# One hybrid decoder layer on one core: reciprocals of the softmax sums taken before they are turned, one weight load traced ahead of the copies, casts behind exponentials, two halves in one step

## The chip, the core and the metric

The kernel runs on one core of a Trainium2 chip. The metric is the device time of one execution in microseconds (us); the time of a kernel is the median of its runs. A core has a matrix engine (PE, with its weight loads shown as PEld), a vector engine (DVE), a scalar engine (ACT), a general engine (POOL) and SyncE (SP), which here mostly issues DMA transfers. Every engine takes its own instructions strictly in the order in which they stand, and waits on semaphores for what the others make.

## The reference

One decoder layer over 1024 positions of width 1024, all float32. Both attention groups read one normalised input; group A has 8 query heads over 2 key heads in a window of 128 with a sink logit, group B has 8 heads with a learned decay.

```python
xn = rmsnorm(x, attn_norm_g)
proj = jnp.einsum('bsd,de->bse', xn, w_in)
qa, ka, va, qb, kb, vb, f_logit = jnp.split(proj, IN_SPLITS, axis=-1)
# q and k of both groups are RMS-normalised per head of 64
out_a = swa_sinks_attention(qa, ka, va, sink_logits)   # exp(s-m) / (sum + exp(sink-m)) @ v
out_b = forgetting_attention(qb, kb, vb, log_f)        # softmax(s + c[t] - c[s]) @ v
x = x + jnp.einsum('bse,ed->bsd', concatenate([out_a, out_b]), w_out)
hn = rmsnorm(x, mlp_norm_g)
hid = jnp.square(jax.nn.relu(jnp.einsum('bsd,df->bsf', hn, w_up)))
return x + jnp.einsum('bsf,fd->bsd', hid, w_down)
```

## The kernel before, in words

Every large product is made of three: an operand is **split** into a rounded high part (a cast, by ACT or DVE) and a low remainder (a subtraction, by DVE or POOL), and high*high, high*low and low*high are added in PSUM. `split` (L75) does it for weights.

The program has these stages.

1. **First projection** (L177 to L227): 8 row tiles (`qps0` to `qps7`, all 8 PSUM banks) of the first 384 columns of the input projection. The results are copied to `q0`, even tiles by DVE and odd ones by ACT (L225 to L227).
2. **Second projection** (`wa1_tile`, L455): 392 more columns, 8 tiles of 24 products each, with weights that `load_w` (L237) brings: for each of 8 slices a DMA into `wr`, a cast `w` by ACT, a low part `w` by POOL. Results go to two PSUM buffers (`ps`, pool `pd`), from which ACT copies them to `q3` and `z`. Meanwhile `qknorm` (L266) squares `q0` and `q3` on POOL (`sq`), sums on DVE (`ss`) and scales on POOL, and the q and k parts are turned by PE (`ptq`, `ptk`, L331) and split (`q1a`, `k1a`, `k2z`).
3. **Attention of group A** (`scores_a`, `mix_a`; 16 units), then **group B** in four pairs of heads p = 0 to 3 (`scores_b`, `mix_b`; 8 units each). A unit makes scores `sp`/`spb` on PE, adds a bias with a running minimum on DVE (`sa`, `sb`, `nm`), an exponential with its sum on ACT, and two units later turns the probabilities on PE (`tpa`, `tpb`, L565 and L740), evicts them split (`pth` by ACT, `ptl` by DVE, L402 and L403), multiplies by v (`pv`, `pvb`) and sends the result (`mta`, `mtb`, two buffers of the tag "mt") to DRAM (`mix_d`). The turned tiles of all these steps, and that of the sums, share **three PSUM buffers of the tag "tr"**. Between them PE works on fillers: the 8 tiles of the next pair's projection (`project_b`, `ps`) and, during p = 3, the first half of the output projection (`out_first`, `po`).
4. **Sums.** For group A and for p = 0 to 2 the probabilities are not divided at once: the sums lie in `dn_a` or `dn_b`, one column for each head and tile of 128 queries. `inverse_to` (L583) turns them on PE (`ptn`), takes reciprocals on DVE (`rd`, tag "mt") and stores them to `rd_d`. `split_mix(e)` (L602) later loads a row block of `mix_d` (`mixr`) and the broadcast reciprocals (`mixn`), and in two steps, one for each half of 512, multiplies them on DVE (L624), splits the product (ACT and POOL, `mixs`) and stores it to `mixs_d`, from where `load_mix` brings it as an operand of the output projection. Pair p = 3 is divided in place (L711 to L718).
5. **Output projection and both MLP products** (from L957): the MLP in a seven-product scheme of 512-column blocks, bound to PE from end to end.

The order on each engine is not written out. The code is traced with priorities (`high_priority`, by which a block is taken earlier), and a scheduler places each instruction when its model of the engines finds it ready. `issue_after(i)` puts the block's instructions that run on i's engine behind i in that engine's order and adds no wait. `PACE` says at which unit a filler is let in, and `SPLITS` after which unit each `split_mix` starts: its load at once, its steps one by one after the next units.

Of the kernel before, what the change touches and what calls it, by code (L numbers as in the profile page):

```python
# [8 lines left out]
F32 = mybir.dt.float32  # L9
# [3 lines left out]
ALU = mybir.AluOpType  # L13
AX = mybir.AxisListType
PSUM = bass.MemoryType.PSUM

P = 128
D = 1024
S = 1024
KT = D // P  # L20
NT = S // P
HD = 64
NH = 8
# [15 lines left out]
LAST = (6, 7, 0, 1, 2, 3, 4, 5)  # L39
# [16 lines left out]
def hybrid_layer(  # L56
# [13 lines left out]
    nc = tc.nc  # L70

    def mm(out, lhsT, rhs, start, stop):
        return nc.tensor.matmul(out, lhsT, rhs, start=start, stop=stop)  # L73

    def split(hi, lo, src, hi_eng, lo_eng):  # L75
        if hi_eng is nc.scalar:
            hi_eng.copy(hi, src)  # L77
        else:
            hi_eng.tensor_copy(hi, src)
        return lo_eng.tensor_tensor(out=lo, in0=src, in1=hi.bitcast(F32), op=ALU.subtract)  # L80

    def rsqrt(pool, out, t, shape, tag):
# [11 lines left out]
    cp = ctx.enter_context(tc.tile_pool(name="cp", bufs=1))  # L94
# [3 lines left out]
        out=ident, in_=ident, pattern=[[-1, P]], compare_op=ALU.not_equal,  # L98
# [4 lines left out]

    vt = cp.tile([P, 68], F32, name="vt")
    gm, vec, bfb, snk = (
        vt[:, a:b] for a, b in ((0, 8), (8, 12), (12, 20), (20, 28))
    )
# [53 lines left out]
    ap2 = at.enter_context(tc.tile_pool(name="ap2", bufs=1, side="right"))  # L163

    ap3 = at.enter_context(tc.tile_pool(name="ap3", bufs=1, side="right"))
    qk_t = lambda name: ap1.tile([P, NT, 384], F32, tag="qk", name=name, bufs=2)
# [10 lines left out]
    st0 = ExitStack()  # L177
    ps0 = st0.enter_context(tc.tile_pool(name="ps0", bufs=1, space=PSUM))
    qps = [ps0.tile([P, 512], F32, name=f"qps{t}") for t in range(NT)]
# [5 lines left out]
    for k in range(KT):  # L185
        xr = ap2.tile([P, S], F32, tag="s", name="xr", bufs=NS)

        wr, wh, wl = w_tiles(384)
# [15 lines left out]
        for cs in pieces:  # L204
# [3 lines left out]
                out=lo, in0=xr[:, cs], scalar=ga,  # L208
# [9 lines left out]
        for t, j in order:  # L218
# [2 lines left out]
                qps[t][:, :384], x_part(part_, k, slice(t * P, (t + 1) * P)), w_,  # L221
                k == 0 and j == 0, k == KT - 1 and j == 2,
            )
    q0 = qk_t("q0")
    for t in LAST:  # L225
        eng = (nc.vector.tensor_copy, nc.scalar.copy)[t % 2]
        eng(q0[:, t, :], qps[t][:, :384])  # L227
    st0.close()

    psa = ExitStack()  # L230
    pa = psa.enter_context(tc.tile_pool(name="pa", bufs=1, space=PSUM, reuse_waits="tile"))
    psd = ExitStack()
    pd = psd.enter_context(tc.tile_pool(name="pd", bufs=2, space=PSUM, reuse_waits="tile"))

    copied, squared = [], []

    def load_w(src, n):  # L237
        his, los = [], []
        for k in range(KT):
            wr, wh, wl = w_tiles(n)  # L240
            nc.sync.dma_start(wr[:, :n], src[:, k, :])
            with ExitStack() as behind:
                for ins in (copied[-1], squared[-1]) if copied and k > 2 else ():
                    behind.enter_context(tc.issue_after(ins))
                behind.enter_context(tc.high_priority(offset=HPO))
                split(wh, wl, wr[:, :n], nc.scalar, nc.gpsimd)
            his.append(wh)
            los.append(wl)
        return his, los

    middle = []

# [13 lines left out]
    def qknorm(x, nh, tlo, thi, r=None):  # L266


        n = thi - tlo
        w = nh * HD  # L270
        ss, r0, u = (
            ap3.tile([P, 16], F32, tag=tag, name=tag, bufs=2)[:, : n * nh]
            for tag in ("ss", "sr0", "su")
        )
        m = n // 2
        for i in range(2):
            sq = ap2.tile([P, 512], F32, tag="sq", name="sq", bufs=1)[:, : m * w]
            xv = x[:, tlo + i * m : tlo + (i + 1) * m, :w]
            square = nc.gpsimd.tensor_tensor(
                out=sq.rearrange("p (t c) -> p t c", t=m), in0=xv, in1=xv, op=ALU.mult  # L280
            )
            if i == 0:
                squared.append(square.ins)
            nc.vector.tensor_reduce(
                out=ss[:, i * m * nh : (i + 1) * m * nh],
                in_=sq.rearrange("p (g d) -> p g d", d=HD), axis=AX.X, op=ALU.add,
            )
        th = lambda a: a.rearrange("p (t h) -> p t h", h=nh)
        nc.vector.scalar_tensor_tensor(
            out=th(ss), in0=th(ss), scalar=1.0 / HD,  # L290
            in1=ep2[:, tlo:thi].unsqueeze(2).to_broadcast([P, n, nh]),
            op0=ALU.mult, op1=ALU.add,
        )
        nc.scalar.activation(r0, ss, AF.Ln)
        nc.scalar.activation(r0, r0, AF.Exp, scale=-0.5)
        nc.vector.tensor_tensor(out=u, in0=r0, in1=r0, op=ALU.mult)
        nc.vector.tensor_tensor(out=u, in0=u, in1=ss, op=ALU.mult)
        na = nh + (2 if r is not None else 0)
        if r is None:
            rv = ap3.tile([P, 16], F32, tag="r", name="r", bufs=2)[:, : n * nh]  # L300
            rv = th(rv)
        else:
            rv = r[:, tlo:thi, :]
        nc.vector.scalar_tensor_tensor(
            out=rv[:, :, :nh], in0=th(u), scalar=3.0, in1=th(r0),
            op0=ALU.subtract, op1=ALU.mult,
        )
        for t in range(n):
            xt = x[:, tlo + t, : na * HD].rearrange("p (h d) -> p h d", d=HD)
            nc.gpsimd.tensor_tensor(  # L310
                out=xt, in0=xt, in1=rv[:, t].unsqueeze(2).to_broadcast([P, na, HD]), op=ALU.mult
            )
# [93 lines left out]
        return hi, lo  # L406


    wa1 = load_w(w_a1, 392)
    rt = cp.tile([P, NT], F32, name="rt")  # L410
    for t in range(NT):
        xq = ap2.tile([P, S], F32, tag="s", name="xq", bufs=NS)
# [114 lines left out]
    def scores_a(g, i):  # L527
        lo = 0 if i else P
        kr = slice(max(i - 1, 0) * P, max(i - 1, 0) * P + 256)
        pts = [  # L530
            ap2.tile([P, 2, 256], F32, tag=("u", "s")[j], name=f"sa{j}", bufs=(NU, NS)[j])
            for j in range(2)
        ]
        nm, dn = (a[:, 4 * g : 4 * g + 4, i] for a in (nm_a, dn_a))
        for h in range(2):
            sp = pa.tile([P, 2, 256], F32, tag="sc", name="sp", bufs=2)
            for j in range(2):
                qs = qa[g, j, i // 4][:, h, (i % 4) * P : (i % 4 + 1) * P]
                mm(sp[:, j, :], qs, k1a[g][:, kr], True, False)
                pe = mm(sp[:, j, :], qs, k2_of[g][:, kr], False, True)  # L540
            for j in range(2):
                hh = 2 * j + h
                n = 256 - lo
                nc.vector.tensor_tensor_reduce(
                    out=pts[j][:, h, lo:], in0=sp[:, j, :n], in1=ab[g][:, hh, lo:],
                    scale=1.0, scalar=nsnk[:, 4 * g + hh : 4 * g + hh + 1],
                    op0=ALU.add, op1=ALU.min, accum_out=nm[:, hh : hh + 1],
                )
        for hh in range(4):
            pr = pts[hh // 2][:, hh % 2, lo:]  # L550
            nc.scalar.activation(
                pr, pr, AF.Exp, scale=-1.0, bias=nm[:, hh : hh + 1],
                accum_out=dn[:, hh : hh + 1],
            )
        marks.append(pe.ins)
        return pts

# [24 lines left out]

    def inverse_to(first, dn, n):  # L583

        pt = pa.tile([P, 512], F32, tag="tr", name="ptn", bufs=3)
        nc.tensor.transpose(pt[: n * NT, :P], dn.rearrange("p h t -> p (h t)"), ident)
        rd = ap2.tile([P, 256], F32, tag="mt", name="rd", bufs=2)[: NH * NT, :P]
        nc.vector.reciprocal(rd[: n * NT], pt[: n * NT, :P])
        nc.sync.dma_start(
            rd_d[first : first + n].rearrange("h (t q) -> (h t) q", q=P), rd[: n * NT]  # L590
        )
# [10 lines left out]
    def split_mix(e):  # L602


        got = {}

        def load():
            for c in range(2):
                cs = slice(c * 512, (c + 1) * 512)
                m, q = got[c] = [  # L610
                    ap2.tile([P, 512], dt, tag=n, name=n, bufs=2)
                    for n, dt in (("mixr", F32), ("mixn", F32R))
                ]
                nc.sync.dma_start(m, mix_d[e][:, cs])
                for h in range(2):
                    nc.sync.dma_start(
                        q[rows_of[h], :].bitcast(F32), rd_d[2 * e + h, cs].partition_broadcast(HD)
                    )

        def make(c):  # L620
            m, q = got[c]
            lo = ap2.tile([P, 512], F32R, tag="mixs", name="mixs", bufs=1)
            with tc.issue_after(mixed[-1]):
                nc.vector.tensor_tensor(out=m, in0=m, in1=q.bitcast(F32), op=ALU.mult)  # L624
            split(q, lo, m, nc.scalar, nc.gpsimd)
            for part_, t in enumerate((q, lo)):
                nc.sync.dma_start(
                    mixs_d[e][part_][:, c * 512 : (c + 1) * 512], t.bitcast(F32)
                )

        return [load, lambda: make(0), lambda: make(1)]


# [784 lines left out]
```

## Time and profile before

| what | value |
|---|---|
| runs | 1082.19, 1083.85, 1083.93 us; median 1083.85 us |
| profiled execution | 1082.51 us, its span 1080.8 us (1.7 us lie around the span) |
| granted PE clock | 0.999 of full speed |
| busy in the span | PEld 930.5, DVE 780.2, ACT 573.4, POOL 383.2 us |
| instructions | PE 5492, DVE 1319, ACT 1022, POOL 350 |
| stages by time in the span | first projection to about 38 us, second to 77, group A to about 200, group B to 427, then output projection to 465, MLP up to 772, MLP down to 1078 |

A timeline row gives the start, the duration from the first start to the last end of a merged group, engine, source line, operation, output tile and inputs, shapes and the count; in brackets stands the idle time ahead of it and what ended it. PE's records overlap: a product's record is longer than the distance to the next product's start, so that PE can count as busy while it loses time. What a stall costs is read from the distance of two starts against the usual one for that shape.

### The profile page before, as it was taken

Reading aid. Unit: us, or ns where it says so; the run is one execution under the profiler, and the core shown is the slowest. Engines: PE = TensorE matmul, PEld = TensorE weight load, DVE = VectorE, ACT = ScalarE, POOL = GpSimd, SP = SyncE. Lnnn points to the kernel's source line nnn. Section 1 sums busy time; section 2 is a strip of 40 time slices with the busy share of each in tenths; the row PEclk is TensorE's granted clock in tenths of the full one; section 3 lists DMA queues with packets and bytes.
Section 4 is the critical chain, followed back from the end, with each engine's and each line's share of the span. In section 5 each row is a group of like instructions: output and inputs, shape, how many; then the busy total and the mean of one; then the engine's idle time right before and its main releaser. Section 6 shows DMA issues by size and latency. Waiting matters only on the chain.

```text
span 1080.8 us, 15581 instructions
## 1 busy us (share of the span) xinstructions
PE 1070.7 (99%) x5492; PEld 930.5 (86%) x5492; DVE 780.2 (72%) x1319; ACT 573.4 (53%) x1022; POOL 383.2 (35%) x350
## 2 busy tenths in 40 slices
PE   9999999999999999999999999999999999999998
PEld 8999999999998887888888888888888888888886
DVE  7377787877875787997777869674776876764495
ACT  5558587776767765655445453534533433333331
POOL 4572433546555663323233332322212313131100
PEclk9999999999999999999999999999999999999999
DMA  8401212324747656544454543443998885665423
GB/s 290 163 20 56 62 43 66 117 89 139 235 169 250 228 193 241 196 156 175 166 202 168 182 169 146 153 162 116 369 391 311 307 296 200 236 232 186 174 81 116
DMA packets 96366, 195.93 MB, mean 181 GB/s; under 512 B 7408, under 2 KB 19872, under 8 KB 96288
## 3 DMA queue, kind: packets, MB, share of 16 engines
q1 hardware_dynamic: 96000, 194.80, 51.2%
q8 instruction: 43, 0.70, 0.3%
q14 instruction: 35, 0.29, 0.1%
q10 hardware_dynamic: 288, 0.15, 0.0%
HBM read 141.87 MB, written 53.04 MB: 180 GB/s over the span
## 4 chain that ended last, share of the span: by engine, by line
PE 72%; DVE 2%; issue 1%; DMA 0%; ACT 0%; DVEq 0%; ACTq 0%
PE pu L73 28%; PE pd L73 28%; PE po L73 8%; PE pvb L73 2%; PE ps L73 2%; PE tpb L740 2%; PE spb L73 2%; DVE ptl L403 0%; DVE sb L699 0%; DMA mix_d<-mtb 0%; PE ptk L331 0%; DVE m L1040 0%; DVE pd L1333 0%; PE ptq L331 0%; PE pms L73 0%
## 5 line engine op out<-in xcount | busy, mean ns | idle before, releaser
L73 PE MATMUL pd<-hx,wx 128*128 128x512 f32 (+1 forms) x1350 | 304.9, 388 | 0.0
L73 PEld LDWEIGHTS pd<-hx,wx 128*128 128x128 f32 x1350 | 252.8, 188 | 52.1
L73 PE MATMUL pu<-bh,wu 128*128 128x512 f32 x896 | 276.6, 390 | 0.0
L73 PEld LDWEIGHTS pu<-bh,wu 128*128 128x128 f32 x896 | 168.2, 188 | 35.2 <-issue 0.2
L73 PE MATMUL ps<-w,x 128*128 128x384 f32 (+1 forms) x960 | 196.5, 342 | 0.6 <-ACT z L460 0.3
L73 PE MATMUL pu<-bl,wu 128*128 128x512 f32 x448 | 174.5, 389 | 0.0
L73 PEld LDWEIGHTS ps<-w,x 128*128 128x128 f32 x960 | 165.2, 188 | 4.8 <-POOL w L80 1.0
L77 ACT CAST hx<-hr 128x1024 fp32r<-128x1024 f32 x56 | 59.1, 1055 | 175.2 <-PE pd L73 171.0
L80 POOL TENSOR_TENSOR wx<-wda,wx 128x1024 fp32r<-128x1024 f32 x24 | 65.3, 2720 | 195.6 <-ACT wx L77 177.3
L80 DVE TENSOR_TENSOR hx<-hr,hx 128x1024 fp32r<-128x1024 f32 x56 | 72.3, 1299 | 71.0 <-ACT hx L77 71.0
L73 PEld LDWEIGHTS pu<-bl,wu 128*128 128x128 f32 x448 | 84.1, 188 | 18.0 <-DVE bl L978 0.3
L73 PE MATMUL po<-mix,wos 128*128 128x512 f32 x384 | 93.6, 393 | 0.0
L80 POOL TENSOR_TENSOR wu<-wus,wu 128x512 fp32r<-128x512 f32 x32 | 46.9, 1468 | 127.5 <-ACT wu L77 127.5
L73 PEld LDWEIGHTS po<-mix,wos 128*128 128x128 f32 x384 | 70.7, 188 | 13.8
L80 POOL TENSOR_TENSOR wu<-wur,wu 128x512 fp32r<-128x512 f32 x31 | 41.8, 1350 | 85.6 <-ACT wu L77 85.6
L77 ACT CAST wu<-wus 128x512 fp32r<-128x512 f32 x64 | 38.0, 618 | 58.9 <-PE pu L73 52.8
L1037 DVE TENSOR_TENSOR ht<-hb 128x512 f32<-128x512 f32 x32 | 22.9, 756 | 63.2 <-ACT hb L1145 63.2
L704 ACT ACTIVATE sb<-sb,nmb 128x128 f32<-128x128 f32 (+3 forms) x64 | 49.9, 779 | 26.3 <-DVE nmb L699 25.7
L403 DVE TENSOR_TENSOR ptl<-tpb,pth 128x512 fp32r<-128x512 f32 (+1 forms) x80 | 49.9, 630 | 17.5 <-ACT pth L402 16.6
L77 ACT CAST wx<-wda 128x1024 fp32r<-128x1024 f32 x56 | 58.5, 1049 | 7.6 <-DMA wda<-in_w_d_dram 7.6
L80 POOL TENSOR_TENSOR w<-wr,w 128x384 fp32r<-128x384 f32 (+1 forms) x47 | 49.9, 1070 | 28.6 <-ACT w L77 17.3
L694 POOL TENSOR_SCALAR_AFFINE_SELECT cm<-cb 128x128 f32<-128x128 f32 (+1 forms) x64 | 30.7, 479 | 57.5 <-DVE nmb L699 56.8
(207 smaller groups left out, 1837.7 us busy)
## 6 DMA issues: line engine op xcount, KB each, us to landing
wda<-in_w_d_dram SPq DMA_DIRECT2D x34, 1024.0 KB, 9.1
hr<-hid_d SPq DMA_DIRECT2D x56, 512.0 KB, 6.3
wur<-in_w_u_dram SPq DMA_DIRECT2D x32, 512.0 KB, 4.4
hid_d<-ht SPq DMA_DIRECT2D x16, 1024.0 KB, 4.3
hid_d<-hb SPq DMA_DIRECT2D x16, 768.0 KB, 3.6
mix<-mixs_d SPq DMA_DIRECT2D x7, 1024.0 KB, 5.8
wr<-in_w_b_dram SPq DMA_DIRECT2D x32, 192.0 KB, 2.4
xq<-in_x_dram SPq DMA_DIRECT2D x8, 512.0 KB, 5.7
```

The source lines that it names most:

```text
L73: return nc.tensor.matmul(out, lhsT, rhs, start=start, stop=stop)
L77: hi_eng.copy(hi, src)
L80: return lo_eng.tensor_tensor(out=lo, in0=src, in1=hi.bitcast(F32), op=ALU.subtract)
L403: nc.vector.tensor_tensor(out=lo[:, cols], in0=pt[:, cols], in1=hi[:, cols].bitcast(F32), op=ALU.subtract)
L694: nc.gpsimd.affine_select(out=cm, in_=bias, pattern=[[-1, n]], compare_op=ALU.is_ge, fill=BIG, base=n - P, channel_multiplier=1,)
L704: nc.scalar.activation(pr[:, :nk], pr[:, :nk], AF.Exp, scale=-1.0, bias=nm[:, c : c + 1], accum_out=dn_b[p % 2][:, h, i : i + 1] if p < 3 ...
L740: nc.tensor.transpose(tp[:, c0 : c0 + P], probs[qi][:, kb * P : (kb + 1) * P], ident)
L1037: eng.tensor_tensor(out=out, in0=a, in1=b, op=ALU.subtract)
```

## The change

Six edits:

- `load_w(w_a1)` is traced ahead of the copies of `q0`, not after them; the copies of tiles 1, 3 and 5 (on ACT) stand behind the last cast of that load, and the first square of `qknorm` (on POOL) behind its last low part.
- In the loads of the pairs' weights, the casts of slices 3 to 7 stand, besides what they stood behind, behind the last exponential of the first unit of group A (`exps[0]`) when it has been traced.
- `inverse_to` takes the reciprocals on DVE on the sums themselves, in place, before they are turned: 128 x 64 for group A and 128 x 16 for a pair, where it was 64 x 128 and 16 x 128 out of PSUM.
- The turned reciprocals are copied out of PSUM by ACT.
- They go to a tile of the tag "zes" (one buffer) and no longer to "mt" (two buffers, shared with `mta` and `mtb`).
- `split_mix(6)` makes both halves in one step. Besides, a constant tile `vt` is 28 and not 68 columns wide, of which 28 were used.

```diff
+    split_casts = []
     def split(hi, lo, src, hi_eng, lo_eng):
-        if hi_eng is nc.scalar:
-            hi_eng.copy(hi, src)
-        else:
-            hi_eng.tensor_copy(hi, src)
+        cast = (hi_eng.copy if hi_eng is nc.scalar else hi_eng.tensor_copy)(hi, src)
+        split_casts[:] = [cast.ins]
...
-                for ins in (copied[-1], squared[-1]) if copied and k > 2 else ():
+                for ins in (copied[-1], squared[-1], *exps[:1]) if copied and k > 2 else ():
...
+    wa1 = load_w(w_a1, 392)
+    last_a1 = list(split_of)
+
+    q0 = qk_t("q0")
+    for t in LAST:
+        eng = (nc.vector.tensor_copy, nc.scalar.copy)[t % 2]
+        with tc.issue_after(last_a1[0]) if t in (1, 3, 5) else nullcontext():
+            eng(q0[:, t, :], qps[t][:, :384])
...
+            with tc.issue_after(last_a1[1]) if not squared else nullcontext():
+                square = nc.gpsimd.tensor_tensor(
...
-    wa1 = load_w(w_a1, 392)
...
+        exps.append(exp.ins)
...
     def inverse_to(first, dn, n):
 
+        nc.vector.reciprocal(dn, dn)
         pt = pa.tile([P, 512], F32, tag="tr", name="ptn", bufs=3)
         nc.tensor.transpose(pt[: n * NT, :P], dn.rearrange("p h t -> p (h t)"), ident)
-        rd = ap2.tile([P, 256], F32, tag="mt", name="rd", bufs=2)[: NH * NT, :P]
-        nc.vector.reciprocal(rd[: n * NT], pt[: n * NT, :P])
+        rd = ap2.tile([P, P], F32, tag="zes", name="rd", bufs=1)
+        nc.scalar.copy(rd[: n * NT], pt[: n * NT, :P])
...
+        if e == KT - 2:
+            return [load, lambda: (make(0), make(1))]
         return [load, lambda: make(0), lambda: make(1)]
```

Three places show how the order moves. The first is POOL at the end of the first projection: `w` of 392 columns are the low parts of the second projection's weights, `sq` the squares of `q0`. Before:

```order
L80 TENSOR_TENSOR w<-wr,w 128x384 x6
L80 TENSOR_TENSOR w<-wr,w 128x392 x7
L279 TENSOR_TENSOR sq<-q_424 128x512
L80 TENSOR_TENSOR w<-wr,w 128x392
L279 TENSOR_TENSOR sq<-q_424 128x512 x2
L310 TENSOR_TENSOR q_424<-q_424,rqk 128x384 x4
```

With the change:

```order
L80 TENSOR_TENSOR w<-wr,w 128x384 x6
L80 TENSOR_TENSOR w<-wr,w 128x392 x8
L285 TENSOR_TENSOR sq<-q_464 128x512 x4
L316 TENSOR_TENSOR q_464<-q_464,rqk 128x384 x4
L285 TENSOR_TENSOR sq<-q_518 128x384
```

The eighth low part no longer stands behind a square, and all four squares of `q0` now stand ahead of its first scaling.

The second place is DVE during the pair p = 2, where the sums of p = 1 are inverted. Before, the reciprocal reads the turned tile `ptn`:

```order
L403 TENSOR_TENSOR ptl<-tpb,pth 128x512
L699 ISA sb,nmb<-spb,cm 128x128
L699 ISA nmb 128x1
L588 RECIPROCAL rd<-ptn 16x128
L403 TENSOR_TENSOR ptl<-tpb,pth 128x384
```

With the change it reads the sums, stands some 45 rows earlier on DVE, and the release of `ptn` is a copy on ACT; the first fence is DVE, the second ACT, whose casts `pth` release the other tiles of the tag:

```order
L409 TENSOR_TENSOR ptl<-tpb,pth 128x512
L591 RECIPROCAL dn_b_83<-dn_b_83 128x16
L409 TENSOR_TENSOR ptl<-tpb,pth 128x384
L764 TENSOR_TENSOR mtb<-pvb,mtb 64x256
L631 TENSOR_TENSOR mixr<-mixr,mixn 128x512
```

```order
L408 CAST pth<-tpb 128x384 x2
L713 ACTIVATE sb,dn_b_82<-sb,nmb 128x512
L595 COPY rd<-ptn 16x128
L656 COPY qkb_3501<-ps 128x384
L408 CAST pth<-tpb 128x512
```

So PE's turning of the sums now waits for DVE, and its tile is given back by ACT.

The third place is DVE near the end of group B, with the second product `mixr` of `split_mix(6)` before:

```order
L713 TENSOR_SCALAR sb<-sb,dnb 128x640
L755 TENSOR_TENSOR mtb<-pvb,mtb 64x256
L624 TENSOR_TENSOR mixr<-mixr,mixn 128x512
L403 TENSOR_TENSOR ptl<-tpb,pth 128x512
L711 RECIPROCAL dnb<-dnb 128x1
```

With the change the second product stands some 19 rows earlier, beside the first (first fence), and around the eviction `ptl` in question (second fence) none is left:

```order
L764 TENSOR_TENSOR mtb<-pvb,mtb 64x256
L631 TENSOR_TENSOR mixr<-mixr,mixn 128x512 x2
L720 RECIPROCAL dnb<-dnb 128x1
L708 ISA sb,nmb<-spb,cb_5147 128x512
L708 ISA nmb 128x1
```

```order
L409 TENSOR_TENSOR ptl<-tpb,pth 128x384
L708 ISA sb,nmb<-spb,cm 128x256
L708 ISA nmb 128x1
L720 RECIPROCAL dnb<-dnb 128x1
L722 TENSOR_SCALAR sb<-sb,dnb 128x768
L409 TENSOR_TENSOR ptl<-tpb,pth 128x512
```

On PE the fillers move with it: before, 12 products `po` stand in two groups of six on either side of eight turnings, now all 12 stand ahead of them:

```order
L73 MATMUL spb<-k2z_441,q1b_4557 128x256
L73 MATMUL po_5721<-mix_4738,wos 128x512 x3
L73 MATMUL po_5721<-mix_5146,wos 128x512 x3
L740 MATMUL tpb<-ident,sb 128x128 x8
L73 MATMUL po_5722<-mix_4738,wos 128x512 x3
L73 MATMUL po_5722<-mix_5146,wos 128x512 x3
```

With the change eleven turnings follow one another:

```order
L73 MATMUL po_5726<-mix_5149,wos 128x512
L73 MATMUL pvb<-pth,vb_4821 128x256
L749 MATMUL tpb<-ident,sb 128x128 x3
L73 MATMUL pvb<-ptl,vb_4821 128x256
L749 MATMUL tpb<-ident,sb 128x128
L73 MATMUL pvb<-pth,vb_4821 128x128
L73 MATMUL pvb<-ptl,vb_4821 128x128
L749 MATMUL tpb<-ident,sb 128x128 x11
```

In the second projection PE's first scores `sp` stand, counted over the rows, behind 99 products `ps` before and behind 115 now. The rest of the order shifts by a few rows throughout group A and group B; behind L957 hardly anything moves.

More of the change, by code (lines that the diff above doesn't have):

```diff
@@ L102, in hybrid_layer @@
     nc.vector.memset(ones1, 1.0)
-    vt = cp.tile([P, 68], F32, name="vt")
+    vt = cp.tile([P, 28], F32, name="vt")
     gm, vec, bfb, snk = (
@@ L223, in hybrid_layer @@
             )
[L224 to L235, printed above, removed]
+    copied, squared, split_of, exps = [], [], [], []
     def load_w(src, n):
@@ L242, in load_w @@
             with ExitStack() as behind:
-                for ins in (copied[-1], squared[-1]) if copied and k > 2 else ():
+                for ins in (copied[-1], squared[-1], *exps[:1]) if copied and k > 2 else ():
                     behind.enter_context(tc.issue_after(ins))
                 behind.enter_context(tc.high_priority(offset=HPO))
-                split(wh, wl, wr[:, :n], nc.scalar, nc.gpsimd)
+                low = split(wh, wl, wr[:, :n], nc.scalar, nc.gpsimd)
+            split_of[:] = [split_casts[0], low.ins]
             his.append(wh)
@@ L249, in load_w @@
         return his, los
+    wa1 = load_w(w_a1, 392)
[5 more added lines that the diff above has]
+            eng(q0[:, t, :], qps[t][:, :384])
+    st0.close()
+    psa = ExitStack()
+    pa = psa.enter_context(tc.tile_pool(name="pa", bufs=1, space=PSUM, reuse_waits="tile"))
+    psd = ExitStack()
+    pd = psd.enter_context(tc.tile_pool(name="pd", bufs=2, space=PSUM, reuse_waits="tile"))
     middle = []
@@ L278, in qknorm @@
             xv = x[:, tlo + i * m : tlo + (i + 1) * m, :w]
-            square = nc.gpsimd.tensor_tensor(
-                out=sq.rearrange("p (t c) -> p t c", t=m), in0=xv, in1=xv, op=ALU.mult
-            )
+            with tc.issue_after(last_a1[1]) if not squared else nullcontext():
+                square = nc.gpsimd.tensor_tensor(
+                    out=sq.rearrange("p (t c) -> p t c", t=m), in0=xv, in1=xv, op=ALU.mult
+                )
             if i == 0:
@@ L550, in scores_a @@
             pr = pts[hh // 2][:, hh % 2, lo:]
-            nc.scalar.activation(
+            exp = nc.scalar.activation(
                 pr, pr, AF.Exp, scale=-1.0, bias=nm[:, hh : hh + 1],
```

## Prediction

> **What bounds the kernel now.** I read first the page's busy times, then the chain that ended last, then the list of PE's waits.
>
> ```profile
> PE 1070.7 (99%) x5492; PEld 930.5 (86%) x5492; DVE 780.2 (72%) x1319; ACT 573.4 (53%) x1022; POOL 383.2 (35%) x350
> ```
>
> PE has 10.1 us of the span in which no record runs. The chain shows where it can't be moved at all:
>
> ```profile
> 426.78 38.16 PE po L73 x168
> ...
> 771.60 300.57 PE pd L73 x1326
> ```
>
> Shown are the first and the last of the four long stretches from 426.8 us on, in which products follow one another with next to nothing between them; 38.16 / 168 is 0.227 us for a product of 512 columns, which is also 300.57 / 1326. Nothing in the change touches these, so the kernel's end lies a fixed distance behind the last product of group B, and the change is worth what it takes from PE's stalls before 427 us, no more. The waits of PE:
>
> ```profile
> PE tpb L740 <- DVE ptl L403: 1.0, 1, 1.0
> PE tpb L740 <- DVE dnb L711: 0.6, 1, 0.6
> PE tpb L740 <- DVE rd L588: 0.6, 1, 0.6
> ...
> PE ps L73 <- ACT z L460: 0.3, 1, 0.3
> PE ps L73 <- POOL w L80: 0.3, 1, 0.3
> PE sp L73 <- DVE q1a L324: 0.3, 1, 0.3
> ```
>
> These are few and short, and three of these six name what the change touches. Their true size is larger, since the records overlap; I take it from the starts. The ceiling of the whole change is thus some 7 us, 0.7% of the time.
>
> **Part 1: the load ahead of the copies.**
>
> ```profile
> L73 PE MATMUL ps<-w,x 128*128 128x392 f32 x192 | 36.6, 346 | 0.6 <-ACT z L460 0.3 <-POOL w L80 0.3
> ...
> 38.36 4.07 PE L73 MATMUL ps<-w,x 128*128 128x392 f32 x22
> 42.70 0.45 PE L73 MATMUL ps<-w,x 128*128 128x392 f32 x1 [0.27 <-POOL w L80]
> ...
> 40.60 1.06 POOL L279 TENSOR_TENSOR sq<-q 128x512 f32<-128x512 f32 x1
> ...
> 41.63 1.01 POOL L80 TENSOR_TENSOR w<-wr,w 128x392 fp32r<-128x392 f32 x1
> ...
> 57.62 0.27 PE L331 MATMUL ptk<-ident,q 128*128 128x128 f32 x1
> 58.15 0.39 PE L73 MATMUL sp<-k1a,q1a 128*128 128x256 f32 x1 [0.26 <-DVE q1a L324]
> ```
>
> The first row is a group (busy us, mean ns of one record): less the 0.35 us of the last record, 22 products follow at (4.07 - 0.35) / 21 = 0.177 us, so the 23rd was due at 42.26 and came at 42.70: **0.4 us** lost, because the eighth low part stood behind a square of 1.06 us on POOL. In the new order it stands ahead of that square, and its cast ahead of two copies on ACT; POOL is free at 40.6, so it is ready near 41.6. I take the 0.4 us as gone. What is late next is the square, by some 1.1 us, and with it the scaling and turning of `q0`. The first scores `sp` came 0.53 us behind the start of a turning, which takes 0.1 at most (eight in 1.03 us, below). In the new order 115 products of the second projection stand ahead of them, where it was 99: 16 x 0.177 = 2.8 us more time for a chain that is 1.1 us later, so I count **0.5 us** as gone too. Bounds: 0 (both come back at the next buffer, as `z` L460 does above) to -0.9.
>
> **Part 2: casts behind exponentials.**
>
> ```profile
> 79.86 0.52 ACT L77 CAST w<-wr 128x384 fp32r<-128x384 f32 x1 [1.55 <-DMA wr<-in_w_b_dram]
> 80.28 0.40 ACT L551 ACTIVATE sa<-sa,nm_a 128x128 f32<-128x128 f32 x1
> ```
>
> ACT stood 1.55 us behind a weight slice that had not landed, with exponentials queued behind it. In the new order the four of the first unit stand ahead of it: 4 x 0.4 = 1.6 us, just the time that ACT stood, so the cast is hardly later than its DMA lets it be. PE's list names a low part `w` once only, that of part 1, and no exponential; I count **nothing**. The cover is PE's fillers; without them 1.6 us would be to gain, or as much to lose if the weights came late.
>
> **Part 3: the reciprocals and their tile.** `ptn` takes one of the three "tr" buffers until the reciprocal has read it.
>
> ```profile
> L588 DVE RECIPROCAL rd<-ptn x4: 935/937/946, 204.9 to 388.0; 16x128 f32<-16x128 f32 x3, 64x128 f32<-64x128 f32 x1
> ...
>   DMA mix_d<-mtb: 0.9, 1
> ...
> 201.76 0.49 PE L740 MATMUL tpb<-ident,sb 128*128 128x128 f32 x3
> 202.43 0.36 PE L73 MATMUL pvb<-pth,vb 128*128 128x256 f32 x1 [0.18 <-DVE mta L576]
> ...
> 255.19 0.27 PE L586 MATMUL ptn<-ident,dn_b 128*16 128x128 f32 x1
> ...
> 269.01 0.94 DVE L588 RECIPROCAL rd<-ptn 16x128 f32<-16x128 f32 x1
> ...
> 269.17 0.70 PE L73 MATMUL ps<-w,x 128*128 128x384 f32 x3
> 270.00 0.55 PE L740 MATMUL tpb<-ident,sb 128*128 128x128 f32 x3
> 270.61 0.38 PE L73 MATMUL pvb<-pth,vb 128*128 128x256 f32 x1
> ...
> 314.36 0.27 PE L586 MATMUL ptn<-ident,dn_b 128*16 128x128 f32 x1
> ...
> 325.97 0.40 PE L73 MATMUL spb<-k2z,q1b 128*128 128x512 f32 x1
> 326.96 0.55 PE L740 MATMUL tpb<-ident,sb 128*128 128x128 f32 x3 [0.60 <-DVE rd L588]
> ```
>
> It is held from 255.19 to 269.95, and from 314.36 to 326.9: 12 to 15 us, because `rd` waits for a buffer of "mt", and so for a store of `mtb`. PE then turns with two buffers. At 326.96 the turning was due 0.23 us after 325.97: 0.77 us lost. At 270.00 three products of 0.174 from 269.17 end at 269.69: 0.3 lost, and 0.3 more ahead of 270.61. Sum **1.4 us**. With the change `rd` has its own buffer, free since the store of a pair before, and ACT's copy stands among the `pth` casts.
>
> ```profile
> L711 DVE RECIPROCAL dnb<-dnb x16: 143/164/165, 357.4 to 415.9; 128x1 f32<-128x1 f32 x16
> ...
> L477 DVE RECIPROCAL zt<-zt x1: 553/553/553, 112.1 to 112.1; 128x64 f32<-128x64 f32 x1
> ...
> L754 ACT COPY mtb<-pvb x32: 369/370/373, 203.5 to 426.9; 64x256 f32<-64x256 f32 x32
> ```
>
> The reciprocals cost 0.55 us for 128 x 64 and, between 0.16 and 0.55, about 0.25 for 128 x 16: 1.3 us in place of 3.75 on DVE. The copies cost at most 0.37 us each, 4 x 0.37 = 1.5 us on ACT, off the path as long as ACT idles. Bounds for the part: 0 (the next buffer is as late) to -1.8, if the gap ahead of 202.43 (0.67 from the turnings' start, where three take 0.25) goes as well, where group A's `ptn` was held too but another release is named. I take -1.4, since a reader of `ptn` is named at the longest gap and ends 0.05 us ahead of the other.
>
> One rule speaks against this part: the Trainium skill, "Perfetto Trace Analysis", section "Optimizing Scalar/DVE Operations", sees offloading from VectorE to ScalarE as sensible when VectorE is saturated, and VectorE is busy 72% here. By it the copy would gain nothing, and the sum would lose its 1.4; the row of `rd` says that the buffer was held by a wait and not by load.
>
> **Part 4: both halves in one step.**
>
> ```profile
> 410.79 1.54 PE L73 MATMUL po<-mix,wos 128*128 128x512 f32 x6
> ...
> 413.92 1.44 DVE L624 TENSOR_TENSOR mixr<-mixr,mixn 128x512 f32<-128x512 f32 x1
> 415.28 0.68 DVE L403 TENSOR_TENSOR ptl<-tpb,pth 128x512 fp32r<-128x512 f32 x1
> ...
> 412.17 1.03 PE L740 MATMUL tpb<-ident,sb 128*128 128x128 f32 x8
> ...
> 416.11 0.52 PE L740 MATMUL tpb<-ident,sb 128*128 128x128 f32 x3 [0.64 <-DVE dnb L711]
> 417.63 1.16 PE L740 MATMUL tpb<-ident,sb 128*128 128x128 f32 x7 [1.00 <-DVE ptl L403]
> ```
>
> PE's two longest waits, by starts 0.86 and 1.17 us, follow from `ptl` at 415.28, which stood behind `mixr`. Without that row it starts near 413.9. But the order of the rest changes with it. Now the pair's last scores are done at 410.8, where the fillers start, and the turning that waits last starts at 417.63, 6.8 us later; without `mixr` 5.4, and with one eviction more in that time, as the new order has it, 6.1. PE then has between the two 12 x 0.227 for the fillers, which now come first, 15 turnings at 0.11 and 12 pv products of half the columns, 0.12 each: 5.8 us. That leaves a wait of 0.3; but the first three of those turnings after eight already need an eviction, and the low part of the result now follows its sum on DVE at once and must stand for ACT's cast, up to 1 us at each place. So the 2.0 us become 0.3 to 2.3. I take 1.5, nearer to the upper end, because both waits ended on DVE: **-0.5**, with bounds +0.3 and -1.7.
>
> **The sum.** -0.4 - 0.5 - 1.4 - 0.5 = -2.8. The order moves by some rows everywhere, and a handful of short waits comes and goes with it; I allow +0.3. That is -2.5 us: 1082.5 - 2.5 = 1080.0 for an execution like the profiled one. The median of the runs stands 1.3 us above that execution, so the median with the change is 1083.85 - 2.5 = **1081.3 us**, 0.23% less.
>
> **Rivals.** (a) *The waits come back at the next buffer*: a `tr` buffer is freed earlier, but the next turning then waits for `ptl` or `mtb`, as the list shows at other places; only part 1's first gap and the 0.77 stay gone, 1.2 us, less 0.3: about 1083.0. For it: DVE is above 70% busy in this stage. Against it: a hold of 12 us is longer than any cast. (b) *The new wait of PE*: the turning `ptn` waits now for DVE, and behind it in PE's order stand scores and fillers. Its slack is short:
>
> ```profile
> 253.57 0.18 ACT L704 ACTIVATION_READ_ACCUMULATOR sb<-sb,nmb 128x1 f32 x1
> ```
>
> The last sum is there at 253.75, the turning runs at 255.19: 1.4 us, into which a reciprocal of 0.25 must fit. If DVE is more than 1.2 us late at that place, PE stops, and everything behind it; two evictions and a score pass (1.9 us) ahead of it would cost 0.7 to 2 us in each of three pairs, 4 us, and take the 1.4 back: 1083.85 + 4 - 1.1 = 1086.8, slower. In the new order the reciprocal stands right among the evictions of that unit, which were waited for before too, so this is unlikely. (c) *All of it goes*: parts 1, 3 and 4 at their bounds, -0.9 - 1.8 - 1.7: 1079.4.
>
> A rule would make (b) worse: the Trainium skill, "SBUF — State Buffer", section "Who interferes with whom", says that a VectorE instruction with two SBUF inputs contends with a GpSimd one that reads SBUF. The trace agrees: `mixr` took 1.44 us above and 0.69 in its median. Two of them in a row can hold DVE 2.9 us; here they stand ahead of a score that PE makes some 3.5 us later.
>
> **How the numbers follow.** My forecast, a gain between 1.3 and 3.7 us, gets 0.5; (a) 0.35; (b) 0.06; (c) 0.09. The range leaves out (b) and a gain beyond that of (c): 1079.2 to 1083.9. A measurement of this kernel tells 0.2%, 2.2 us, from no change. The forecast lies close to that line: of its 0.5, 0.4 is beyond it, with (c) 0.49 faster; (a) and the rest, 0.44, within; (b) and a little of (a) 0.07 slower.
>
> **What would show it.** Right: PE's start after the 22nd product without a gap; no wait of `tpb` on a reader of `ptn`, which is free within 2 us; `mixr` twice in a row near 400 us and no `mixr` in the last chain; at the end a `tpb` wait of 1 to 2 us on `ptl`. Wrong: PE waiting at `ptn` for DVE; new waits above 0.5 us in the second projection; the sum of the gaps before 427 us unchanged.

## The result, and the profile after

| kernel | runs | median | ratio to before, 95% interval |
|---|---|---|---|
| before | 1082.19 to 1083.93 us (4) | 1083.84 us | 1 |
| with the change | 1092.58 to 1097.18 us (4) | 1094.03 us | 1.0106 [1.0094, 1.0118] |

The kernel is 10.2 us slower. Forecast were 1081.3 us, in a range of 1079.2 to 1083.9: the time lies outside of it, on the other side.

The profiled execution is the slowest of the four, with 1097.18 us and a span of 1095.5, which is 14.7 more than the span before. First the busy times of the page, to be read against those before in the prediction:

```profile
PE 1083.1 (99%) x5492; PEld 933.0 (85%) x5492; DVE 772.0 (70%) x1319; ACT 576.7 (53%) x1026; POOL 384.9 (35%) x350
```

PE is busy 12.4 us longer with as many instructions; DVE is busy 8.2 us less, and PEld, ACT and POOL 1.7 to 3.3 us more. The chain that ended last says where PE's time goes. First the stretch that the prediction left out of its rows, MLP up of the kernel before (start, us, products):

```profile
464.94 190.65 PE pu L73 x840
655.59 1.72 PE pms L73 x4
657.31 114.29 PE pu L73 x504
```

Then the same chain with the change, from the output projection to MLP down:

```profile
431.29 38.16 PE po L73 x168
469.45 196.79 PE pu L73 x840
666.25 1.72 PE pms L73 x4
667.96 118.08 PE pu L73 x504
786.04 300.82 PE pd L73 x1326
```

`po` takes 38.16 us in both. The 1344 products `pu` of MLP up take 196.79 + 118.08 = 314.87 us, where it was 304.94: **9.9 us more**, without one new wait. 114.29 / 504 is 226.8 ns for a product, 118.08 / 504 is 234.3: each is 7.5 ns slower. `pd` loses 0.25 us. That makes 10.2 us, as much as the whole difference of the medians. The other 4.5 us of this execution lie ahead of 431.29 us, where before stood 426.78; another execution of the same attention code (`a28pad`, its row below) reached this point at 428.00, so most of them belong to this execution. One cause is in its trace: from 421.1 to 424.6 us the granted PE clock is 0.5, which costs some 1.7 us (an estimate: half of that length); in the profiled execution of before it is full from the first products to 1079.6 us, just ahead of the end.

The waits of PE, with the change, are those that were foretold to go and others in their place:

```profile
PE tpb L749 <- DVE ptl L409: 3.0, 4, 1.4
...
PE sp L73 <- DVE nm_a L549: 1.1, 3, 0.6
PE ptq L337 <- DVE ptl L409: 1.0, 1, 1.0
PE spb L73 <- DVE nmb L708: 0.7, 2, 0.6
```

No wait on `rd` or `dnb` is left, but evictions `ptl` and running minima are waited for more than before.

Nothing that the change does to the order reaches MLP up. One edit does: `vt` became 40 columns narrower, 160 bytes, and all tiles that are allocated behind it on the left side of SBUF lie 160 bytes lower. The addresses in the built programs (bytes in a partition; `wu` is the stationary operand of `pu`, `bh` and `bl` the moving ones; the tiles of one kind stand at multiples of 512 bytes from each other):

```
                 lowest wu  bh1      distance   past a multiple of 256
before           69856      108512   38656        0
with the change  69696      108512   38816      160
```

Of the long stretches only MLP up is moved so: in both programs all products of `po` and `pd` lie at multiples of 256 bytes, and these two stages keep their rate.

### The profile page after: what moved, and what is told of

Read it like the earlier page. It is cut to its first block, busy times and chain, and to the rows that moved or that the text cites. A ratio compares the mean times of both kernels' runs of the same rounds, so it can differ in the third digit from the quotient of the medians.

```text
span 1095.5 us, 15587 instructions
## 1 busy us (share of the span) xinstructions
PE 1083.1 (99%) x5492; PEld 933.0 (85%) x5492; DVE 772.0 (70%) x1319; ACT 576.7 (53%) x1026; POOL 384.9 (35%) x350
## 4 chain that ended last, share of the span: by engine, by line
PE 89%; DMA 4%; DVE 3%; issue 1%; ACT 1%; POOL 1%; SPq 0%; POOLq 0%; ACTq 0%; DVEq 0%
PE pu L73 29%; PE pd L73 27%; PE ps L73 14%; PE po L73 6%; PE pvb L73 3%; PE spb L73 3%; PE tpb L749 2%; PE pv L73 1%; PE sp L73 1%; PE tpa L571 1%; DMA xq<-in_x_dram 1%; DMA wor<-in_w_o_dram 1%; DVE x L207 1%; PE ptk L337 1%; PE ptq L337 1%
## 5 line engine op out<-in xcount | busy, mean ns | idle before, releaser
L73 PE MATMUL pu<-bh,wu 128*128 128x512 f32 x896 | 283.3, 397 | 0.0
L73 PE MATMUL pu<-bl,wu 128*128 128x512 f32 x448 | 177.6, 396 | 0.0
L80 DVE TENSOR_TENSOR hx<-hr,hx 128x1024 fp32r<-128x1024 f32 x56 | 75.3, 1351 | 76.8 <-ACT hx L78 76.8
L749 PE MATMUL tpb<-ident,sb 128*128 128x128 f32 x288 | 46.7, 278 | 3.1 <-DVE ptl L409 3.0
```

The lines of the kernel that those rows point to most:

```text
L749: nc.tensor.transpose(tp[:, c0 : c0 + P], probs[qi][:, kb * P : (kb + 1) * P], ident)
```

## Experiments

### Is it the place, and what about the place?

`b28` is the kernel before with the narrow `vt` alone; `a36` the changed kernel with 36 columns; `a28pad` and `b68pad` move the other operand, with a tile that nothing uses:

```diff
# b28: before
-    vt = cp.tile([P, 68], F32, name="vt")
+    vt = cp.tile([P, 28], F32, name="vt")
# a36: changed kernel
-    vt = cp.tile([P, 28], F32, name="vt")
+    vt = cp.tile([P, 36], F32, name="vt")
# a28pad: changed kernel, b68pad: before
     rr = o["zr"].tile([P, S], F32, name="rr")
+    o["zr"].tile([P, 8], F32, name="rpad")
```

> The kernel before with `vt` 28 columns wide, and nothing else: the tiles of the left side lie 160 bytes lower, at a multiple of 64. Theory A (place): 234 ns from start to start in the MLP-up stage, 316.6 us for it, and about 1094 in all. Theory B (order): 227 ns, 306.6 us, 1084.

> The changed kernel with `vt` 36 columns wide in place of 28: every tile of the left side lies 32 bytes further on, at 32 past a multiple of 64 as before the change, and nothing else differs. Theory A (place in SBUF: a product of the MLP-up stage is slow when its stationary and its moving operand lie differently against 64 bytes): the 1344 products start every 227 ns again, the stage takes 306.6 us and the kernel about 1084, 10 us less than the changed one. Theory B (the new order of the work, by way of the other engines or the DMAs, slows this stage): still 234 ns, 316.6 us, and 1094.

> The changed kernel with an unused tile of 32 bytes behind `rr` in the right side's pool of the MLP: the moving operands bh and bl go down by 32 bytes to a multiple of 64, where the stationary wu lies already. Theory A (the two must lie alike against 64 bytes): 227 ns, 306.6 us for the MLP-up stage, about 1084. Theory A' (a stationary operand at a multiple of 64 is slow by itself): 234 ns, 1094. Theory B (order): 234 ns, 1094.

> The kernel before with the same unused tile of 32 bytes: wu stays at 32 past a multiple of 64, bh and bl go to a multiple of 64. Theory A (alike or not): slow, 234 ns, 316.6 us for the MLP-up stage, about 1094. Theory A'' (only a stationary operand at a multiple of 64 beside a moving one at 32 is slow): 227 ns, 1084. Theory B (order): 227 ns, 1084.

Measured, beside before at 1083.21 us (9 runs): `b28` 1093.74, ratio 1.0094 [1.0076, 1.0111]; `a36` 1090.91, 1.0073 [1.0060, 1.0086]; `a28pad` 1092.41, 1.0087 [1.0065, 1.0109]; `b68pad` 1092.26 in one run. The second stretch of MLP up in the chain, of `b28`, then `a36`, `a28pad` and `b68pad`:

```profile
668.05 118.08 PE pu L73 x504
```

```profile
662.79 117.12 PE pu L73 x504
```

```profile
428.00 38.16 PE po L73 x168
...
663.10 117.12 PE pu L73 x504
```

```profile
663.63 117.59 PE pu L73 x504
```

`b28` has the order of before and the 118.08 us of the changed kernel, to the hundredth: the place does it, and theory B, the order, falls. But theory A falls too: `a36` and `a28pad`, foretold at 227 ns, stay at 117.12 / 504 = 232.4. What they have in common is neither address but the distance: 38784 bytes, made once by moving `wu` up and once by moving `bh` down, gives the same time. `b68pad` is slow, 233.3 ns, as theory A had it, but that fits any theory of the distance as well. So theory C: the distance counts.

### The distance put back

```diff
# a28p160: changed kernel; b28p160: before with vt of 28 columns
     rr = o["zr"].tile([P, S], F32, name="rr")
+    o["zr"].tile([P, 40], F32, name="rpad")
```

> The changed kernel with an unused tile of 160 bytes behind `rr` in the right side's pool of the MLP: bh and bl lie 38656 bytes above the first wu tile again, as before the change, though both lie 160 bytes lower. Theory C (what counts is the distance in SBUF between the moving and the stationary operand, since the kernels tried so far took 226.7 ns for a product at a distance of 38656, 232.4 at 38784 by both ways of making it, 233.3 at 38624 and 234.3 at 38816): 226.7 ns, 306.6 us for the MLP-up stage, and 1082 to 1085 in all, where what is left beside before is the order of the work: the prediction's -2.5 us would make it 1081. Rival (each of the two addresses counts by itself): above 230 ns.

> The kernel before with `vt` 28 columns wide and the same unused tile of 160 bytes: the order of before, the layout of the kernel named just ahead. Theory C: 226.7 ns in the MLP-up stage, and the time of before within 1 us unless the layout also costs something in the attention. Its difference to the kernel named just ahead is the new order of the work alone: -2.5 us for the changed order by the prediction, 0 by the rival that the waits come back at the next buffer.

Beside before at 1083.11 us (29 runs): `a28p160` 1084.57, ratio 1.0010 [0.9998, 1.0023]; `b28p160` 1083.47, 1.0002 [0.9992, 1.0012]. The stretch in `a28p160`, and in `b28p160`:

```profile
662.63 114.29 PE pu L73 x504
```

```profile
658.00 114.29 PE pu L73 x504
```

114.29 us as before, though all operands lie 160 bytes lower than they did. Theory C stands, its rival falls, and with the layout mended the loss of 10 us is gone. What is left for the new order is 1084.57 - 1083.47 = 1.1 us, which these intervals can't tell from nothing; the forecast of -2.5 us for it, a ratio of 0.9977, lies outside of the interval of `a28p160`.

### Which distances

```diff
# curve2: changed kernel (curve: 32 bytes behind each bh and each bl)
         bl[n] = slot(f"c{2 * i + 1}", f"bl{n}", [4, 512], F32R, "zr")
+        o["zr"].tile([P, (16, 16, 32, 64, 64, 128, 96)[i] // 4], F32, name=f"pad{n}")
```

> The changed kernel with an unused tile of 32 bytes behind each of the 14 slots of bh and bl, so that they lie, against the wu tiles, at 480, 0, 32, 64 and so on to 384 bytes past a multiple of 512. Theory C: products are as slow as their distance makes them: about 233 ns at 224, 227 at 256, 232 at 384, and 227 at 0 if the pattern repeats each 256 bytes. Rival (only equal places against 512 or more are fast): slow at 0 also or slow at 256.

> The changed kernel with unused tiles between the pairs of bh and bl, so that both tiles of a pair lie alike against the wu tiles: 480, 0, 32, 64, 128, 192 and 320 bytes past a multiple of 512 for the pairs 1, 2, 3, 6, 7, 5 and 4. Theory C with a period of 256 bytes (fast at 256 so far): 227 ns at 0, above 230 at 480, 32, 64, 192 and 320, and 232 at 128 as at 384. Rival (256 is fast for another reason, and 0 is the worst, the two operands meeting in the same place): above 230 at 0.

In `curve` (1090.57 us, one run) the two operands of a pair lay at different distances, 32 bytes apart, and their products take turns. All pairs took 231 to 234 ns. The two places foretold at 227 were missed: `bl1` at 0 took 231.0 and `bl7` at 256 took 233.0. One reading is that a slow product beside it drags the fast one along; it is not shown, and that kernel tells nothing about single places. `curve2` (1090.54 us, one run) gives both of a pair one distance. The mean time from one start to the next in the trace, ns, by the distance modulo 256, with the kernels above:

```
  0   226.8  before, a28p160, b28p160     (512 x n in curve2: 226.5 to 226.7 in the last 7 of each 12)
 32   233.5  curve2
 64   229.8  curve2    229.3 at 320
128   231.7  curve2    232.4 a36, a28pad (at 384)
160   234.3  the changed kernel, b28
192   234.0  curve2
224   233.8  curve2 (at 480)    233.3 b68pad
```

Distances that are 256 bytes apart agree to within 0.7 ns, and of those tried only a multiple of 256 is fast. A program that mixes several, as `curve2`, needs some products to settle: at 0 the first five behind the pair at 480 still took 228 to 236. Over the last 7 of each 12, as the row of 0 is taken, the others of `curve2` are 233.7 at 32, 229.3 at 64, 232.4 at 128, 233.0 at 192, 229.2 at 320 and 233.5 at 480, and distances 256 bytes apart agree to 0.2 ns. The rival, that 0 is the worst place, falls; 64 and 320, foretold above 230, came out just below.

### Where the gain of the order went

With the distance put back, parts were taken out of `a28p160`: part 4 (`a28p160no4`), 2 and 4 (`a28p160no24`), 3 and 4 (`a28p160no34`), and all but part 3 (`b28p160only3`).

```diff
# no4
-        if e == KT - 2:
-            return [load, lambda: (make(0), make(1))]
# no24: also
-                for ins in (copied[-1], squared[-1], *exps[:1]) if copied and k > 2 else ():
+                for ins in (copied[-1], squared[-1]) if copied and k > 2 else ():
# no34: no4, and rd as before
-        nc.vector.reciprocal(dn, dn)
...
-        rd = ap2.tile([P, P], F32, tag="zes", name="rd", bufs=1)
-        nc.scalar.copy(rd[: n * NT], pt[: n * NT, :P])
+        rd = ap2.tile([P, 256], F32, tag="mt", name="rd", bufs=2)[: NH * NT, :P]
+        nc.vector.reciprocal(rd[: n * NT], pt[: n * NT, :P])
# only3: no24, and load_w(w_a1), the copies of q0 and the first square where they were
```

> The changed kernel with the 160 bytes and without part 4 (the last head group's halves are made in two steps again). By the prediction part 4 is worth -0.5 us (+0.3 to -1.7), so this would take 0.5 us more than with it. Rival: part 4 costs 2 to 4 us, since three new waits of PE on evictions stand between 412 and 422 us of the changed kernel's trace (0.74, 1.60 and 1.23 us); then this is faster than the kernel before, near 1081.

> The changed kernel with the 160 bytes and without parts 2 and 4 (parts 1 and 3 stay). By the prediction's terms parts 1 and 3 take 2.3 us from the order of before: 1081.2 against the 1083.5 of the kernel with that order and this layout. Rival (part 2 is not free: the three waits of the scores on `nm_a` at 77, 81 and 82 us of the kernel with all parts, 1.5 us by starts against 0.6 before, come from the exponentials moved ahead of the casts): the waits near 80 us shrink to 0.6 and the time falls by 1 us against the kernel without part 4 only, 1084.6. Rival (parts 1 and 3 give back later what they gain): no change, 1083.5 to 1084.6, with the gain's loss visible between 400 and 430 us.

> The order of before with part 3 alone (reciprocals of the sums ahead of their turning, `rd` in a buffer of its own), with `vt` of 28 columns and the 160 bytes. By the prediction's term of part 3: 1.4 us less than the 1083.5 of the same layout without it, 1082.1, and no wait of `tpb` on `rd`. Rival (a): the next buffer waits as long, 1083.5.

> Parts 1 and 2 on the order of before (parts 3 and 4 left out), with `vt` of 28 columns and the 160 bytes. In the traces so far parts 1 and 2 remove the stalls near 43, 58 and 68 us, 1.4 us, and bring 0.8 us of waits on `nm_a` near 80 us: 0.6 us less than the 1083.5 of the same layout without them, about 1083, with `tpb` waiting on `rd` and on `dnb` as before. Rival (the time saved at 43 to 68 us is lost again before 430 us, where the projection's weights or the last evictions set the pace): 1083.5 to 1084.5.

| parts | kernel | median | ratio to before, 95% interval |
|---|---|---|---|
| none | b28p160 | 1083.47 us | 1.0002 [0.9992, 1.0012] |
| 3 | b28p160only3 | 1084.64 | 1.0007 [0.9998, 1.0015] |
| 1, 2 | a28p160no34 | 1083.28 | 1.0004 [0.9995, 1.0014] |
| 1, 3 | a28p160no24 | 1086.44 | 1.0026 [1.0014, 1.0037] |
| 1, 2, 3 | a28p160no4 | 1084.64 | 1.0012 [1.0000, 1.0025] |
| 1 to 4 | a28p160 | 1084.57 | 1.0010 [0.9998, 1.0023] |

The ratios go by the runs of before made beside each: 1083.11 us for the rows without parts, with parts 1 to 3 and with all, 1083.83 for those with 3 and with 1 and 3, 1083.51 for that with 1 and 2. No combination beats the kernel before. Of the forecasts, `a28p160no34` came out near its 1083; `a28p160no24` and `b28p160only3` missed theirs, 1081.2 and 1082.1, by 5.2 and 2.5 us. Part 4 shows no effect: with and without it the medians are 0.07 us apart, which can't tell its 0.5 us from nothing, but the rival, 2 to 4 us lost by it, falls. Only one row is clearly slower than before, and a pair of rows shows a cause. Without part 2, ACT and then PE near 80 us (`a28p160no24`):

```profile
79.64 0.51 ACT L78 CAST w<-wr 128x384 fp32r<-128x384 f32 x1 [2.32 <-DMA wr<-in_w_b_dram]
80.06 0.40 ACT L556 ACTIVATE sa<-sa,nm_a 128x128 f32<-128x128 f32 x1
...
80.60 0.48 PE L571 MATMUL tpa<-ident,sa 128*128 128x128 f32 x1 [2.10 <-ACT sa L556]
```

With part 2, in `a28p160`:

```profile
77.24 0.40 ACT L556 ACTIVATE sa<-sa,nm_a 128x128 f32<-128x128 f32 x1
...
79.38 0.51 ACT L78 CAST w<-wr 128x384 fp32r<-128x384 f32 x1 [0.48 <-DMA wr<-in_w_b_dram]
```

The same cast waits for its weights; without part 2 it holds the exponentials up from about 77 to 80.06 us, and PE stands 2.1 us for them. (That it came early by part 1 is the likely reason: `b28p160only3`, without parts 1 and 2, has no such wait.) The rival that part 2 costs time is not borne out: 1.0026 without it, 1.0012 with it, with intervals that overlap.

The stall is not the whole loss. From 79.7 to 86.5 us the granted PE clock of that execution is 0.5, where it is full in `a28p160`. The products of the projection start every 0.32 us there and every 0.17 here; first `a28p160no24`, then `a28p160`:

```profile
81.73 2.76 PE L73 MATMUL ps<-w,x 128*128 128x384 f32 x8
```

```profile
78.75 1.73 PE L73 MATMUL ps<-w,x 128*128 128x384 f32 x9
```

6.8 us at half the clock cost up to 3.4 us (an estimate), more than the stall itself. Stretches like it, of 3.4 or 6.8 us, stand in the traces of five kernels between 416 and 426 us, within 2 us of the end of a wait of PE: the changed kernel, `b28`, `a28p160no4`, `a28p160no24` and `b28p160only3`. The mean granted clock over all runs is 0.9972 in `a28p160no24` and 0.9975 in `a28p160no4`, and 0.9988 in the runs of before beside each; that alone makes some 1.7 and 1.4 us (an estimate: that share of the time), against 2.8 and 1.3 by their ratios. Which waits bring the clock down is not shown: `a28p160` has waits of 1.46 and 1.02 us near 420 us, and its profiled execution keeps the full clock.

Part 3 alone does what it says and gives it back. PE and DVE in `b28p160only3`, in the unit where the kernel before waited for `ptl` and `dnb`:

```profile
413.47 1.78 PE L743 MATMUL tpb<-ident,sb 128*128 128x128 f32 x11
417.16 0.39 PE L73 MATMUL pvb<-pth,vb 128*128 128x256 f32 x1 [1.92 <-DVE mtb L758]
...
415.96 0.16 DVE L714 RECIPROCAL dnb<-dnb 128x1 f32<-128x1 f32 x1 [1.09 <-ACT sb L707]
416.16 0.62 DVE L716 TENSOR_SCALAR sb<-sb,dnb 128x768 f32<-128x768 f32 x1
416.70 0.41 DVE L758 TENSOR_TENSOR mtb<-pvb,mtb 64x256 f32<-64x256 f32 x1
```

Its list of waits names neither `rd` nor `dnb` at any `tpb`, but DVE stands 1.09 us for the sum of an exponential, with the eviction `mtb` queued behind, and PE waits for that. By starts the one wait costs 417.16 - 413.47, less 11 turnings at 0.11 and the 0.3 that the last one takes longer to end, about 2.2 us, where the two of before cost 2.0. Another stands at 332 us:

```profile
PE ptq L332 <- DVE ptl L404: 1.1, 1, 1.1
```

Behind the wait at 417.16 us the granted clock is 0.5 from 417.5 to 420.9. The median is 1.2 us above that of the same layout without part 3, with overlapping intervals: the 1.4 us were not gained.

## Why the prediction was wrong

**The failed step** stands in its first paragraph on the bound: "Nothing in the change touches these, so the kernel's end lies a fixed distance behind the last product of group B". The order of MLP up is indeed untouched, and no wait came into it; but the rate of its products was taken as given, 0.227 us. The narrow `vt`, named in the change and priced nowhere, moved `wu` against `bh` and `bl` and made it 0.234: +9.9 us, four times the sum that was forecast. None of the three rivals contained it; all of them stayed ahead of 427 us. Shown by `b28` (that edit alone, 1.0094) and `a28p160` (all edits, with the distance put back, 1.0010).

Point by point for the rest, with the distance put back:

- *Part 1, -0.9.* The gap ahead of the scores went; the first one, behind the 22nd product, went only where the second projection began late enough. In `a28p160` it begins with 68 products in one piece:

```profile
39.33 12.25 PE L73 MATMUL ps<-w,x 128*128 128x392 f32 x68
...
63.14 0.43 PE L73 MATMUL ps<-w,x 128*128 128x392 f32 x1
63.40 0.28 PE L73 MATMUL sp<-k1a,q1a 128*128 128x256 f32 x1
```

 (12.25 - 0.35) / 67 is 0.178, no stall, and `sp` follows without one. But it begins at 39.33, where it was 38.36. In `a36`, the same order, it begins at 38.22, and the 23rd product waits 0.39 us for POOL's `w` and comes at 42.67: the eighth low part, foretold for 41.6 us, ends there at 42.6. In the time nothing was seen: parts 1 and 2 together are 1.0004, against 1.0002 without, each known to about 1 us. A part of it comes back near 80 us as waits on the running minima; first `b28p160`, then `a28p160no34` with parts 1 and 2:

```profile
PE sp L73 <- DVE nm_a L544: 0.5, 1, 0.5
```

```profile
PE sp L73 <- DVE nm_a L549: 0.9, 2, 0.6
```

- *Part 2, nothing.* It was measured only beside part 1. Beside part 3, part 1 without it costs about 2 us (1.0007 to 1.0026); with it 1.0012 was measured, some 1.5 us less, with intervals that overlap. The sentence on its cover named a price, 1.6 us; it did not see that part 1 may take the cover away.
- *Part 3, -1.4.* The mechanism holds: in PE's list no `tpb` waits for a reader of `ptn` any more, and `ptn` is held for 0.6 to 2.3 us, where it was 8.9 to 14.8. No gain was measured, as in the bound "the next buffer is as late".
- *Part 4, -0.5.* Measured 1.0010 with, 1.0012 without: no effect that these runs could show. The condition that it named, new waits on evictions behind the fillers, came true: `tpb` waits on `ptl` four times, up to 1.4 us, in the list of after, and once, 0.4 us, without part 4 (`a28p160no4`), where one `pvb` stands 1.9 us for `mtb` instead.
- Of the rivals, (a), the waits come back, is nearest to what the order alone does: 1.1 us above the same layout, where (a) had -0.9. (b), PE waiting at `ptn` for DVE, does not appear in any list. The rule weighed against the copy on ACT, as the prediction worked it out, would have given -1.1 for the sum, still on the wrong side, since no term of it was on the layout.

## What to carry to other kernels

A change of a tile's size is a change of the address of all that is allocated behind it: compare the rate of the products, stage by stage, and not only the waits, when a kernel that is bound to PE gets slower without a new stall. In a stage of back-to-back products like these, keep the distance between the moving and the stationary operand a multiple of 256 bytes, and where a tile shrinks, pad. And a stall that is removed ahead of a chain with other evictions close behind counts as gained only when the next release is earlier too. Look at the granted clock stretch by stretch as well: in five of these traces PE ran at half of it for some microseconds close to a stall.

## What was not expected of the hardware

A float32 product (of operands rounded to fp32r) of 128x128 by 512 columns starts every 226.8 ns when its moving operand lies a multiple of 256 bytes from the stationary one, and every 229.3 to 234.3 ns at the other distances tried: up to 3.3%. With both operands 160 bytes lower it is 226.8 again. PE shows no idle time in it; only the weight loads stand longer between each other, with 188 ns for a load in both kernels. The rows of `bh` before, then with the change (the last number is the idle time, us):

```profile
L73 PE MATMUL pu<-bh,wu 128*128 128x512 f32 x896 | 276.6, 390 | 0.0
L73 PEld LDWEIGHTS pu<-bh,wu 128*128 128x128 f32 x896 | 168.2, 188 | 35.2 <-issue 0.2
```

```profile
L73 PE MATMUL pu<-bh,wu 128*128 128x512 f32 x896 | 283.3, 397 | 0.0
L73 PEld LDWEIGHTS pu<-bh,wu 128*128 128x128 f32 x896 | 168.8, 188 | 41.3 <-issue 0.2
```

Why 256, and whether it is the load of the next weights that meets the stream of columns, no run here shows; other shapes and types were not tried.
